# First quarter of the conditioning columns on TensorE, and filter steps issued ahead of it

## The chip, the cores and the metric

One core of a Trainium2 chip runs the program. The metric is device time in microseconds of the whole program, from three runs of each kernel. A profile of one further execution gives durations of single instructions; times inside it count from the start of its span.

## The reference

A trunk of two layers over 256 tokens of width 1024, all fp32. Of each layer only this matters here:

```
cond = silu(c)
ada  = cond @ w_ada[l] + b_ada[l]          # 6 x 1024: shift, scale, gate; twice
u    = x * (1 + scale1) + shift1
proj = u @ w_in[l]                         # attention, Hyena input, gates
filter: h = sin(freq0*(z@w1+b1)); h = sin(freq1*(h@w2+b2))
        h = (h@w3) * exp(-t * exp(log_decay)); normalised, then rfft
```

Attention, the Hyena convolution with these filters, the gates and a channel mixer over 16384 experts follow. The opening of layer 0 can make no u before the first columns of `ada` (shift and scale) are there.

## The kernel before

Weights come as tiles of 128x1024 from HBM on SP's queue (`raw`, three buffers, class `Stream`). ScalarE rounds each to `hi` (L88), VectorE or GpSimd (POOL) makes the rest `lo` (L90, by the letter "v" or "g" given in `plan`), and TensorE takes three products: hi with the high part of u, lo with it, hi with its low part (`tok_mm`, L211).

The opening is `start` (L276). It works in four quarters `kp` of the inner dimension, 256 rows of u each. A quarter's weights of `w_ada` for shift and scale are two tiles `su` of 1 MB (five buffers). For each quarter

* `sums` has VectorE multiply eight 128x512 pieces by one number of `cond` per partition and add them up into two accumulators (L293 twice, L296 six times);
* `columns` has TensorE turn the two accumulators, by products with the identity (L304, 8 matmuls, which the trace shows as 16 passes, since a fp32 matmul takes two), VectorE reduce them (L307) and add the bias (L309, `adac`);
* `u_part` (L479), called for both halves of the tokens, has TensorE turn x (L489), ScalarE make the high part (L492), and VectorE or ScalarE with POOL the low part `ul` (L497, L495, L500);
* `products(5, kp)` and `products(4, kp)` are the 12 matmuls each of two of the column chunks of `w_in`, numbers 5 and 4; chunk 4 comes one quarter late, between the next `columns` and its own `u_part`.

Between these stand steps of a generator, `filters` (L557), which `bg.pump` advances one yield at a time: the two sine layers (L584 on TensorE, seven small steps L587 to L593 on VectorE, L598 on ScalarE), then log_decay as a load spread over all partitions (1 MB) and its Exp (L610), eight products with w3 (L618) multiplied by the decays (L621, L623, L626), squares and their sums (L633 to L647), later the spectra (L676). What of it is not done in the opening goes on behind it, among chunks 0 to 3 of `w_in`.

Each engine works its instructions in the order of the program; the order is the one in which the Python code emits them, and the framework sets the waits. DMAs are issued by SP and by ScalarE's queue.

## Time and profile before

| | us |
|---|---|
| median of 3 runs | 2363.2 (2361.52 to 2363.59) |
| the profiled execution, its own time | 2362.55 |
| its span | 2360.4 |
| TensorE matmuls busy | 2267.1 |
| VectorE busy | 1789.6 |
| ScalarE busy | 1165.5 |
| POOL busy | 301.1 |

Durations and starts below are those of the profiled execution, whose span is 2.15 us shorter than its time. Matmuls are pipelined: a busy TensorE is not one at its peak, and a group of matmuls is read from the start of the first to the start of what follows. "PE" is TensorE, "DVE" VectorE, "ACT" ScalarE; a q behind the name is the engine's queue of DMA issues. An idle engine shows the releaser in brackets, with the idle time before it.

### The profile page before, as it was taken

To read this page: it belongs to the slowest core of one execution; us is meant where nothing else is said; L and a number is where in the kernel's file an instruction comes from. 1 tells how busy PE (TensorE), PEld (TensorE's weight loads), DVE (VectorE), ACT (ScalarE), POOL (GpSimd) and SP (SyncE) were. 2 spreads that over 40 slices of the span, in tenths; PEclk is the share of its full clock that TensorE was granted. 3 is DMA by queue.
4 is the path that set the end of the run, shared out by engine and by line. 5 is a ranking of instruction groups with operands and counts; after the bars stand their busy time and mean duration, and the time that the engine had idled before them with its cause. 6 is when DMAs were issued, how large, how long until landed. Compare 5 with 4: busy or idle time off the path is not lost.

```text
span 2360.4 us, 38122 instructions
## 1 busy us (share of the span) xinstructions
PE 2267.1 (96%) x14400; PEld 1998.4 (85%) x14400; DVE 1789.6 (76%) x3414; ACT 1165.5 (49%) x1850; POOL 301.1 (13%) x177
## 2 busy tenths in 40 slices
PE   6999988999999999999999999999999999999997
PEld 4688767999999988886777987799999999888786
DVE  6886797967778877778886858877777888755656
ACT  3544434555554544444455454555555554444443
POOL 3100004730000000003023000258000000000200
PEclk9999999999999999999999999999999999999999
DMA  8553554555555578888655424455555555766664
GB/s 289 178 171 102 182 202 154 168 179 166 166 167 164 162 242 265 269 268 266 219 189 185 133 93 149 163 155 178 171 168 163 168 164 185 236 193 195 213 200 149
DMA packets 132591, 438.43 MB, mean 186 GB/s; under 512 B 16369, under 2 KB 17741, under 8 KB 130360
## 3 DMA queue, kind: packets, MB, share of 16 engines
q1 hardware_dynamic: 103328, 377.01, 50.5%
q10 hardware_dynamic: 26968, 51.23, 6.3%
q0 software_dynamic: 2112, 7.77, 1.1%
q8 instruction: 113, 1.85, 0.3%
q14 instruction: 70, 0.57, 0.1%
HBM read 432.80 MB, written 3.15 MB: 185 GB/s over the span
## 4 chain that ended last, share of the span: by engine, by line
PE 77%; DVE 14%; ACT 3%; issue 3%; DMA 2%; POOL 0%; ACTq 0%; DVEq 0%
PE bg L223 33%; PE pj L1565 26%; PE pj L211 8%; DVE lo L90 4%; ACT hi L88 2%; PE gp L1463 1%; PE gp L1464 1%; PE pj L223 1%; PE bg L676 1%; DVE acc L432 1%; PE bg L618 1%; PE pj L1032 1%; PE pj L1376 1%; DMA raw<-in_wout 1%; DMA raw<-in_v 1%
## 5 line engine op out<-in xcount | busy, mean ns | idle before, releaser
L90 DVE TENSOR_TENSOR lo<-raw,hi 128x1024 fp32r<-128x1024 f32 x614 | 757.9, 1237 | 336.3 <-ACT hi L88 331.2
L88 ACT ACTIVATE hi<-raw 128x1024 fp32r<-128x1024 f32 x688 | 726.6, 1058 | 457.4 <-PE pj L1565 255.1
L1565 PE MATMUL pj<-hi,P 128*128 128x512 f32 x2048 | 638.8, 393 | 4.3 <-ACT P L1509 2.0
L223 PE MATMUL bg<-uh,hi 128*128 128x256 f32 x2240 | 640.8, 286 | 0.0
L223 PE MATMUL bg<-uh,lo 128*128 128x256 f32 x2240 | 634.1, 283 | 1.8 <-DVE lo L90 1.3
L223 PE MATMUL bg<-ul,hi 128*128 128x256 f32 x2240 | 633.3, 283 | 0.0
L1565 PEld LDWEIGHTS pj<-hi,P 128*128 128x128 f32 x2048 | 384.7, 189 | 90.2 <-ACT hi L88 3.4
L223 PEld LDWEIGHTS bg<-uh,lo 128*128 128x128 f32 x2240 | 429.2, 192 | 3.4 <-DVE lo L90 2.5
L223 PEld LDWEIGHTS bg<-ul,hi 128*128 128x128 f32 x2240 | 429.4, 192 | 0.1
L223 PEld LDWEIGHTS bg<-uh,hi 128*128 128x128 f32 x2240 | 429.3, 192 | 0.1
L1565 PE MATMUL pj<-lo,P 128*128 128x512 f32 x1024 | 401.7, 392 | 7.2 <-DVE lo L90 7.2
L1565 PEld LDWEIGHTS pj<-lo,P 128*128 128x128 f32 x1024 | 193.4, 189 | 51.7 <-DVE lo L90 11.6
L211 PE MATMUL pj<-hi,uh 128*128 128x512 f32 x432 | 189.9, 440 | 3.8 <-DVE mt L1189 2.3
L90 POOL TENSOR_TENSOR lo<-raw,hi 128x1024 fp32r<-128x1024 f32 x74 | 183.6, 2496 | 77.8 <-ACT hi L88 77.5
L1494 ACT ACTIVATE bg<-bg 128x8 f32<-128x8 f32 (+23 forms) x192 | 51.0, 266 | 268.1 <-PE bg L223 268.1
L211 PE MATMUL pj<-lo,uh 128*128 128x512 f32 x432 | 175.0, 405 | 7.2 <-DVE lo L90 7.2
L211 PE MATMUL pj<-hi,ul 128*128 128x512 f32 x432 | 174.9, 405 | 6.4 <-DVE ul L1249 5.7
L197 POOL DMA_DIRECT2D x<-spill x2 | 1.3, 649 | 1117.9 <-DVE P L1510 1117.9
L1470 DVE SCALAR_TENSOR_TENSOR b<-gp,b 128x160 f32<-128x160 f32 (+5 forms) x244 | 63.6, 322 | 97.0 <-ACT b L1468 97.0
L432 DVE SCALAR_TENSOR_TENSOR acc<-adaw,cond,acc 128x512 f32<-128x512 f32 x140 | 110.7, 791 | 0.0
L1079 POOL TENSOR_TENSOR e<-early,e 128x1024 fp32r<-128x1024 f32 x12 | 30.9, 2573 | 620.0 <-ACT e L1078 620.0
L211 PEld LDWEIGHTS pj<-hi,uh 128*128 128x128 f32 x432 | 84.4, 195 | 29.1 <-issue 7.4
(317 smaller groups left out, 2856.2 us busy)
## 6 DMA issues: line engine op xcount, KB each, us to landing
raw<-in_u SPq DMA_DIRECT2D x256, 512.0 KB, 3.6
raw<-in_v SPq DMA_DIRECT2D x256, 512.0 KB, 4.3
raw<-in_wtok SPq DMA_DIRECT2D x92, 512.0 KB, 3.7
adaw<-in_wada ACTq DMA_DIRECT2D x160, 256.0 KB, 4.0
raw<-in_whyd SPq DMA_DIRECT2D x24, 512.0 KB, 3.6
raw<-in_wq SPq DMA_DIRECT2D x24, 512.0 KB, 3.7
raw<-in_wbr SPq DMA_DIRECT2D x20, 512.0 KB, 3.6
su<-in_wada SPq DMA_DIRECT2D x8, 1024.0 KB, 10.6
```

The costliest lines, as they stand in the source:

```text
L88: self.nc.scalar.activation(out=h, in_=t, func=AF.Copy)
L90: eng.tensor_tensor(out=w, in0=t, in1=h.bitcast(F32), op=ALU.subtract)
L211: self.nc.tensor.matmul(psums[T], l[:, k, s], m[:, kk, :], start=(k == 0 and j == 0), stop=(k == K - 1 and j == 2))
L223: self.nc.tensor.matmul(ps, m[:, k, :], x[:, k, :], start=(k == 0 and j == 0), stop=(k == 7 and j == 2))
L432: nc.vector.scalar_tensor_tensor(out=acc, in0=w, scalar=self.cond[:, k:k + 1], in1=acc, op0=ALU.mult, op1=ALU.add)
L618: nc.tensor.matmul(p, hcur[:, T * 128:T * 128 + 128], w3[:, n * 512:n * 512 + 512], start=True, stop=True)
L676: nc.tensor.matmul(ps[P], self.fwd[:, P, c, :], z[:, P, :], start=True, stop=True)
L1032: self.nc.tensor.matmul(ps[T], x[:, 2 * i + kk, ts], w[:, kk, :], start=x is self.uh and i + kk + part == 0, stop=x is self.ul and i + kk ...
L1079: self.nc.gpsimd.tensor_tensor(out=w, in0=t, in1=h.bitcast(F32), op=ALU.subtract)
L1470: nc.vector.scalar_tensor_tensor(out=t[:, :, ts], in0=pr[:, i:j, :], scalar=1.0 / GATE_UNIT, in1=t[:, :, ts], op0=ALU.mult, op1=ALU.mult)
L1494: nc.scalar.activation(out=p[:, 0:n], in_=p[:, 0:n], func=AF.Gelu)
L1565: self.nc.tensor.matmul(self.vacc[T][h], x[:, s], v[:, w], start=start and c == 0, stop=stop and c == 2)
```

## The change

For the first quarter VectorE's sums go. TensorE multiplies the `su` tiles as weights by one column of `cond` (L312, 32 matmuls of one column), and two additions on VectorE make `adac`. For the other quarters the accumulators are summed by a product with a column of ones (L307, 8 matmuls) in place of the turning and the reduce. The log-decay is loaded as one row and spread by four products with a row of ones (L602), each followed by an Exp. Filter steps are advanced by two before the first quarter, by one in it and by two more ahead of each quarter's products. `products(4, kp)` comes right behind `products(5, kp)` and the next `sums`. All low parts of u go to VectorE, as do the two first splits of `w_in` tiles; the other six go to POOL. Only two `raw` tiles are loaded ahead of x. The layer's constants are loaded in quarters 2 and 3.

```diff
--- before.py
+++ after.py
@@ -61,8 +61,8 @@
         self.items.append((key, ap, split, own))
         self.ring.append(self.ring[-1] + (not own))
 
-    def _load(self):
-        while self.n_load < min(self.n_split + self.bufs + self.spare, len(self.items)):
+    def _load(self, most=1000):
+        while self.n_load < min(self.n_split + self.bufs + self.spare, len(self.items), most):
             here = self.where[self.n_split:].count(self.raw_pool) < self.bufs
             self.where.append(self.raw_pool if here else self.own)
             t = self.where[-1].tile([128, 1024], F32, tag="raw", name="raw", bufs=self.bufs if here else self.spare)
@@ -255,6 +255,8 @@
         self.load(self.ident, a["ident"])
         self.bcol = c.tile([128, DEPTH, 6, 8], F32, name="bcol")
         self.load(self.bcol, a["bada"])
+        self.one = c.tile([128, 128], F32, name="one")
+        nc.vector.memset(self.one, 1.0)
         self.new_x()
         self.open_layer(0)
         self.cond = c.tile([128, 8], F32, name="cond")
@@ -297,16 +299,24 @@
                                                        op0=ALU.mult, op1=ALU.add)
                 return acc
 
-            def columns(kp, acc):
-                q = self.bp((128, 4, 128))
+            def columns(kp):
+                q = self.bp((128, 2, 4))
                 for m in range(4):
-                    for i in range(2):
-                        nc.tensor.matmul(q[:, m, :], acc[i][:, m * 128:m * 128 + 128], self.ident,
-                                         start=(i == 0), stop=(i == 1))
-                p = self.sm.tile([128, 2, 2], F32, tag="ac0", name="ac0")
-                nc.vector.tensor_reduce(out=p.rearrange("p j k -> p (j k)"), in_=q, op=ALU.add, axis=AX.X)
+                    ms = slice(m * 128, m * 128 + 128)
+                    for i in range(2 if kp else 0):
+                        nc.tensor.matmul(q[:, 0, m:m + 1], acc[i][:, ms], self.one[:, 0:1], start=(i == 0),
+                                         stop=(i == 1))
+                for i in range(0 if kp else 2):
+                    for m in range(4):
+                        for kk in range(4):
+                            nc.tensor.matmul(q[:, i, m:m + 1], tiles[i][:, kk, m * 128:m * 128 + 128],
+                                             self.cond[:, 4 * i + kk:4 * i + kk + 1], start=(kk == 0), stop=(kk == 3))
                 ks = slice(2 * kp, 2 * kp + 2)
-                nc.vector.tensor_tensor(out=self.adac[:, 0, 0:2, ks], in0=p, in1=self.bcol[:, 0, 0:2, ks], op=ALU.add)
+                p = self.adac[:, 0, 0:2, ks]
+                q = q.rearrange("p i (j k) -> p i j k", j=2)
+                nc.vector.tensor_tensor(out=p, in0=q[:, 0], in1=self.bcol[:, 0, 0:2, ks], op=ALU.add)
+                if not kp:
+                    nc.vector.tensor_tensor(out=p, in0=q[:, 1], in1=p, op=ALU.add)
 
             def load_x(kp):
                 s = slice(kp * 256, kp * 256 + 256)
@@ -315,33 +325,37 @@
             load()
             load()
             load_x(0)
-            st._load()
+            st._load(2)
             for kp in range(1, 4):
                 load_x(kp)
                 load()
             pairs = {n: self.pair() for n in (5, 4)}
             loads = self.layer_loads(0)
-            st.run(3)
-            acc = sums(0)
+            self.bg.pump(2)
+            st.run(2)
 
             def products(n, kp):
                 self.tok_mm(pairs[n], self.uh, self.ul, st.get(("tok", 0, n, kp)), 2 * kp, 2, 8)
                 self.bg.pump()
-                next(loads, None)
+                if kp > 1:
+                    next(loads, None)
+                    next(loads, None)
 
             for kp in range(4):
-                columns(kp, acc)
+                columns(kp)
+                if kp == 0:
+                    self.bg.pump()
                 for T in range(2):
-                    self.u_part(T, 2 * kp, "va"[T], "vg"[T])
+                    self.u_part(T, 2 * kp, "va"[T], "v")
+                self.bg.pump(2)
+                for _ in range((2, 1, 0, 0)[kp]):
+                    load()
+                products(5, kp)
                 if kp < 3:
                     acc = sums(kp + 1)
-                for _ in range((2, 1, 0, 0)[kp]):
-                    load()
-                if kp:
-                    products(4, kp - 1)
-                self.bg.pump()
-                products(5, kp)
-            products(4, 3)
+                products(4, kp)
+            for _ in loads:
+                pass
         return pairs
 
     def new_x(self):
@@ -361,7 +375,7 @@
             if l == 0:
                 for kp in range(4):
                     for n in (5, 4):
-                        st.add(("tok", l, n, kp), a["wtok"][l, n, kp], "g")
+                        st.add(("tok", l, n, kp), a["wtok"][l, n, kp], "g" if kp else "v")
                 tok(0, 1, 2, 3)
             else:
                 tok(5, 4, 1, 2, 3)
@@ -576,8 +590,17 @@
             self.load(nt, a["negt"])
             w3 = fp.tile([64, 2048], F32, name="w3")
             ld = fp.tile([128, 2048], F32, name="ld")
+            if l == 0:
+                row = free[0:1, 1024:3072]
+                self.load(row, a["log_decay"][l:l + 1])
+                self.load(w3, a["hy_w3"][l])
             for _ in range(3 if l else 1):
                 yield
+            if l == 0:
+                for n in range(4):
+                    p = self.bp()
+                    nc.tensor.matmul(p, self.one[0:1, :], row[:, n * 512:n * 512 + 512], start=True, stop=True)
+                    nc.scalar.activation(out=ld[:, n * 512:n * 512 + 512], in_=p, func=AF.Exp)
             hcur, wcur = zt, w1
             for i in range(2):
                 p = self.bp((64, 256))
@@ -600,14 +623,13 @@
                 if l:
                     yield
                 hcur, wcur = h, w2
-            self.load(w3, a["hy_w3"][l])
             if l:
+                self.load(w3, a["hy_w3"][l])
                 yield
-            n = 1024 if l else 2048
-            for i in range(0, 2048, n):
-                self.load(ld[:, i:i + n], a["log_decay"][l][i:i + n].partition_broadcast(128))
-                yield
-            nc.scalar.activation(out=ld, in_=ld, func=AF.Exp)
+                for i in range(0, 2048, 1024):
+                    self.load(ld[:, i:i + 1024], a["log_decay"][l][i:i + 1024].partition_broadcast(128))
+                    yield
+                nc.scalar.activation(out=ld, in_=ld, func=AF.Exp)
             sums = fp.tile([128, 2, 4], F32, name="sums")
             yield
             todo = None
```

Line numbers of the changed kernel: L312 and L307 are the matmuls in `columns`, L317 and L319 its additions, L295 and L298 the sums, L602 the spreading of log-decay, L640 and L645 (L648 the last) the products with w3, L503, L506, L511 and L514 the steps of `u_part`, L610 to L616 the argument steps of a sine.

**TensorE, from its first instruction.** Before (acc are the accumulators of the first quarter):

```order
L304 MATMUL bg<-ident,acc_176 128x128
L304 MATMUL bg<-ident,acc_177 128x128
L304 MATMUL bg<-ident,acc_176 128x128
L304 MATMUL bg<-ident,acc_177 128x128
L304 MATMUL bg<-ident,acc_176 128x128
L304 MATMUL bg<-ident,acc_177 128x128
L304 MATMUL bg<-ident,acc_176 128x128
L304 MATMUL bg<-ident,acc_177 128x128
L489 MATMUL bg<-ident,x 128x128 x4
L584 MATMUL bg<-hh,w_109 64x256
L211 MATMUL pj<-hi,uh 128x512
```

With the change (hh holds the row of log-decay, one the ones, w_111 and w_113 are the filter's w1 and w2):

```order
L602 MATMUL bg<-hh,one 128x512 x4
L607 MATMUL bg<-hh,w_111 64x256
L312 MATMUL bg<-cond,su 128x1 x32
L607 MATMUL bg<-h_181,w_113 64x256
L503 MATMUL bg<-ident,x 128x128 x4
L211 MATMUL pj<-hi,uh 128x512
```

Five products of the filter now stand ahead of the first columns, and another between them and the first turned x.

**VectorE, from the second filter product or reduce of a quarter to the next quarter's sums.** Before, around the third quarter (acc_380 is an accumulator of the fourth):

```order
L307 TENSOR_REDUCE ac_359<-bg 128x4
L309 TENSOR_TENSOR adac<-ac_359,bcol 128x2x2
L497 TENSOR_SCALAR uft<-bg,adac 128x128 x2
L500 TENSOR_TENSOR ul<-uft,uh 128x2x128
L293 TENSOR_SCALAR acc_380<-su,cond 128x512
```

With the change, around the second quarter (acc_287 is an accumulator of the second quarter, acc_379 of the third):

```order
L298 SCALAR_TENSOR_TENSOR acc_288<-su,cond,acc_288 128x512
L645 TENSOR_TENSOR hh<-bg,hh 128x512
L317 TENSOR_TENSOR adac<-bg,bcol 128x2x2
L511 TENSOR_SCALAR uft<-bg,adac 128x128 x2
L514 TENSOR_TENSOR ul<-uft,uh 128x2x128 x2
L645 TENSOR_TENSOR hh<-bg,hh 128x512 x3
L295 TENSOR_SCALAR acc_379<-su,cond 128x512
```

The reduce is gone; a second ul and three products of the filter have come between the columns and the next sums.

**POOL, from the start.** Before:

```order
L90 TENSOR_TENSOR lo<-raw,hi 128x1024 x3
L500 TENSOR_TENSOR ul<-uft,uh 128x2x128 x2
L90 TENSOR_TENSOR lo<-raw,hi 128x1024 x2
L500 TENSOR_TENSOR ul<-uft,uh 128x2x128
L90 TENSOR_TENSOR lo<-raw,hi 128x1024 x2
L994 CAST iota<-iota_437 128x128
L500 TENSOR_TENSOR ul<-uft,uh 128x2x128
L90 TENSOR_TENSOR lo<-raw,hi 128x1024
```

With the change:

```order
L90 TENSOR_TENSOR lo<-raw,hi 128x1024 x5
L649 MEMSET hh 1x1024
L90 TENSOR_TENSOR lo<-raw,hi 128x1024
L1016 CAST iota<-iota_559 128x128
L1114 MEMSET kT 128x3584
```

Three of the eight splits before are ready at the first quarter; of the six now, two belong to each of the later quarters.

## Rows read from the trace of the kernel before

**Rows 1.** The page, the chain that ended last, shares by engine.

```profile
PE 77%; DVE 14%; ACT 3%; issue 3%; DMA 2%; POOL 0%; ACTq 0%; DVEq 0%
```

**Rows 2.** Busy time by stretch: us, engines, granted clock, DMA share, GB/s.

```profile
14.00:16.00 2.00, 2.00 (x9) 1.84 (x10) 0.36 (x1) 1.63 (x2) 1.35 (x1) 1.00 1.03 368
...
20.00:40.00 20.00, 15.07 (x59) 10.53 (x60) 18.38 (x31) 6.50 (x14) 5.55 (x4) 1.00 0.97 385
...
40.00:42.00 2.00, 1.94 (x9) 1.70 (x10) 1.86 (x6) 0.00 (x0) 0.00 (x0) 0.53 0.00 0
```

**Rows 3.** Timeline, TensorE and VectorE, turned sums and stored columns (start, us, what).

```profile
13.75 4.02 PE L304 MATMUL bg<-ident,acc 128*128 128x128 f32 x16 [13.75 <-DVE acc L296]
18.53 0.82 DVE L309 TENSOR_TENSOR adac<-ac,bcol 128x4 f32<-128x4 f32 x1
26.64 2.40 PE L304 MATMUL bg<-ident,acc 128*128 128x128 f32 x16
30.55 0.16 DVE L309 TENSOR_TENSOR adac<-ac,bcol 128x4 f32<-128x4 f32 x1
39.86 3.87 PE L304 MATMUL bg<-ident,acc 128*128 128x128 f32 x16 [3.99 <-DVE acc L296]
44.50 0.16 DVE L309 TENSOR_TENSOR adac<-ac,bcol 128x4 f32<-128x4 f32 x1
55.29 2.05 PE L304 MATMUL bg<-ident,acc 128*128 128x128 f32 x16
58.11 0.16 DVE L309 TENSOR_TENSOR adac<-ac,bcol 128x4 f32<-128x4 f32 x1
```

**Rows 4.** Timeline, TensorE, the narrowest fp32 matmuls that the trace has.

```profile
159.13 1.00 PE L823 MATMUL bg<-v,pt 128*128 128x64 f32 x8
```

**Rows 5.** Timeline, POOL, two splits of the opening.

```profile
34.13 2.38 POOL L90 TENSOR_TENSOR lo<-raw,hi 128x1024 fp32r<-128x1024 f32 x1 [0.20 <-ACT hi L88]
...
48.68 2.36 POOL L90 TENSOR_TENSOR lo<-raw,hi 128x1024 fp32r<-128x1024 f32 x1 [0.21 <-ACT hi L88]
```

**Rows 6.** VectorE groups by line, 34.9 to 35.6, then 23.3 to 24.0.

```profile
L296 DVE SCALAR_TENSOR_TENSOR acc<-su,cond,acc 128x512 f32<-128x512 f32 x1 | 2.9, 2924 | 0.0
...
L296 DVE SCALAR_TENSOR_TENSOR acc<-su,cond,acc 128x512 f32<-128x512 f32 x2 | 1.4, 742 | 0.0
```

**Rows 7.** Chain of waits in order of time, 55 to 80 us (start, us).

```profile
60.52 1.91 PE bg L618 x4
...
66.42 2.96 PE pj L211 x12
69.38 1.05 PE bg L618 x2
...
74.66 1.05 PE bg L618 x2
```

**Rows 8.** Timeline, VectorE, ScalarE and its queue, single steps.

```profile
6.15 0.36 ACTq L197 DMA_DIRECT2D nt<-in_negt  x1
...
27.08 0.53 DVE L587 TENSOR_SCALAR hh<-bg,col 64x256 f32<-64x256 f32 x1
29.63 0.28 DVE L593 TENSOR_SCALAR hh<-hh 64x256 f32<-64x256 f32 x1
43.49 1.04 ACT L88 ACTIVATE hi<-raw 128x1024 fp32r<-128x1024 f32 x1
43.80 0.60 ACTq L197 DMA_DIRECT2D ld<-in_log_decay  x1
47.07 0.42 DVE L500 TENSOR_TENSOR ul<-uft,uh 128x256 fp32r<-128x256 f32 x1
66.55 1.23 DVE L90 TENSOR_TENSOR lo<-raw,hi 128x1024 fp32r<-128x1024 f32 x1 [0.55 <-ACT hi L88]
67.69 0.68 DVE L623 TENSOR_TENSOR hh<-bg,hh 128x512 f32<-128x512 f32 x1
```

**Rows 9.** DMA issues, 0 to 80 us: nt, its KB and the us to landing.

```profile
nt<-in_negt ACTq DMA_DIRECT2D x1, 1.0 KB, 1.7
```

## The prediction

> **What bounds the kernel now.** I read the chain of waits first, for the whole span and then for the opening. Over the span it is 77% TensorE [rows 1], all engines are in-order, and nothing later waits for a fixed hour: a shift of the opening should reach the end almost whole. So the question is when the opening ends. The stretches come second: the transfers fill 0.97 of the DMA engines from 20 to 40 us, but nothing moves from 40 to 42 us [rows 2], while two of the four quarters are still to come; the weights are not the pace there. The timeline names the pace [rows 3]. Four times TensorE turns VectorE's sums (L304), VectorE stores the columns (L309), and only then can the next quarter of u be made. The columns are stored at 19.35, 30.71, 44.66 and 58.27 us (start plus duration). From 55 to 78 us the chain stays on TensorE without a gap, and its last products of the opening end at 69.38 us [rows 7].
>
> **The first quarter.** Sums(0) on VectorE and L304 go. In their place stand, one behind the other on TensorE: the log-decay row, four L602, one L607 and 32 L312.
>
> The row for L602 is issued on ScalarE's queue behind nt, which was issued at 6.15 to 6.51 us and took 1.7 us to land [rows 8, 9]; behind it that gives 8.3 us. (This issue and that of w3, at most 0.60 us each by [rows 8], also put the conditioning vector at most 1.2 us later. It is wanted only by L312, so that is hidden.)
>
> L602 is a fp32 matmul of 512 columns, as L618, of which two take 1.91 us [rows 7], 0.95 each. That is at TensorE's upper pace. L304 shows two paces: 4.02 us for 16 passes in the first quarter, 2.05 us in the fourth [rows 3]. The clock row reads 0.53 beside the 3.87 us of the third quarter; beside the first it reads 1.00, though the passes are as slow [rows 2, 3], so here I go by durations: half pace, 1.2 GHz, at first. Four L602 at half pace are 4 x 0.95 x 1.96 = 7.4 us, L607 with half the columns 0.9 us: 16.6 us.
>
> L312 has one column. Its price is not in the trace. The nearest row has 64 columns: 8 passes in 1.00 us [rows 4], 0.125 each, as much as the 0.128 of L304's 128 columns. Narrow matmuls are not cheaper; every pass has its own 128x128 weight load. 32 matmuls of two passes are 64 passes: 8.2 us at the upper pace, 16.1 at half.
>
> In the kernel before, TensorE ran at half pace from its first matmul at 13.75 until about the second L304, which is fast at 26.64 [rows 3]. I let it run as long at half pace here: 8.3 + 12.9 = 21.2. So 4.6 us of L312 at 0.25 are 18 passes and the other 46 take 5.9: 27.1, and two small additions, 0.16 each plus hand-over, 27.6 us. Against 19.35 that is **+8.2 us**. Bounds: upper pace throughout, 8.3 + 3.8 + 0.5 + 8.2 + 0.5 = 21.3 (+2); half pace throughout, 33.2 (+14). The other engines would not allow much below 24: L610 to L616, seven steps worth 2.83 us (27.08 to 29.91), two L88 of 1.04 and two splits of 1.23 now stand ahead of L317 [rows 8].
>
> **The second quarter**, 11.36 us before. The argument steps lie beside VectorE's sums in both kernels and cancel. New: both w_tok splits of a quarter are now on POOL during the sums. Such a split takes 2.4 us [rows 5], and the accumulation that met one took 2.92 us where its neighbours take 0.74 [rows 6]: VectorE stood still, 2.2 us a time. Before, the second quarter met none, the third and fourth one each. Now I count two in each: +4.4. The second ul moves from POOL to VectorE, 0.42 [rows 8]. L307 has as many passes as L304, so 2.05 us, and it is no longer covered by the argument steps, which now come ahead of the sums: +2.05, less 0.7 for the reduce that stood between L304 and L309 [rows 3]. **+6.2 us.**
>
> **The third quarter.** One more hold, +2.2; ul, +0.4; three L645 of 0.68 [rows 8] now stand between ul and the sums, +2.0; the reduce, -0.7. TensorE idled ahead of L304 here and went to half pace (3.87 us); it will idle again, so L307 costs as much. **+3.9 us.** **The fourth** is the same less the L623 that stood ahead of its reduce, 0.7: **+3.2 us.** The columns are then stored at about 28, 45, 63 and 80 us.
>
> **After the fourth quarter**, 69.38 - 58.27 = 11.1 us before, with two sets of products, L618 and the last set behind. Now: ul is ready 2.83 us after the columns (44.66 to 47.49 [rows 3, 8]), the first set runs into that and ends after some 4.8 us, the second 2.96 later [rows 7]: 7.7. **-3.4 us.**
>
> **Filter steps that no longer follow.** Three L618 behind the opening, 1.05 us each, on the chain [rows 7], and three L623 and L626 of 0.68 us on VectorE [rows 8]: 5.2 at most, 2.0 at least. I take **-5.0**; the squares are the same work a little earlier. Hidden at no cost: Exp in four pieces (ScalarE idles), the one-column memset, the layer's constants issued later (wanted by rope, which comes later too), the raw tiles and su tiles behind them on SP: su for quarter 3 is asked for when L312 ends, near 28 us, and wanted near 50. If that cover were gone, the next late thing would be that tile.
>
> **Sum:** 8.2 + 6.2 + 3.9 + 3.2 - 3.4 - 5.0 = +13.1 us. The profiled execution took 2362.55 us (span 2360.4); its time is 0.65 us below the median of the runs, which is within their spread. 2362.55 + 13.1 = **2375.7 us, slower.** The forecast's own range takes the first quarter at 24 instead of 27.6 (-3.6) and one hold fewer in two quarters (-4.4), or half pace through most of L312 (+5) and through two L307 (+4): 2367 to 2385.
>
> **Rivals.**
>
> *Columns of one are nearly free.* If a one-column pass cost only its issue, L312 would end with the splits on VectorE, at 24 us (-3.6), and L307 would save up to 2.05 us three times (-6.2): +3.3, 2365.9 us, within 0.2%. For it: nothing in the trace is narrower than 64 columns. Against: 64 columns cost what 128 do [rows 4]. The Trainium skill ("TensorE: Matmul & The Clock Gate", section "Wait — 56ns, not 53.3ns?") states that start-to-start never falls below about 25 ns however narrow a matmul is; 64 passes would then be 1.6 us, an estimate, and the total about this rival's. The same page (section "LDWEIGHTS (loading the stationary operand)") prices a weight load by its columns over 1.2, 107 ns for 128, and the 0.125 us of [rows 4] sides with that one. Chance 0.08.
>
> *POOL's splits miss the sums.* They start when ScalarE has made hi, and ScalarE now has Exp steps in front. Each hold that falls elsewhere gives back 2.2 us; without the four added ones, +13.1 - 8.8 = +4.3, about 2366.9 us. For: order on ScalarE is tight. Against: the sums last 5 us and more, and the splits come right behind uh and two Exp in each quarter. In part (two missed, 2371) it lies in my range. Chance of all four 0.09.
>
> *VectorE is what the opening waits for, and it is relieved* (faster). Sums(0), 5 us, and four reduces of 0.7 leave VectorE. If sums(1) could run while L312 does, the second quarter would come at its old 30.7 us, and the quarters after it no later than before; then the -3.4 and -5.0 remain: 2354.2 us. It decides if the fourth columns stand before 58.27 + 8.4 = 66.7 us. For it: TensorE waited 4.0 us for such sums ahead of the third quarter [rows 3]. Against: on VectorE's order sums(1) stands behind the splits, both ul and the second argument steps, all after L317. Chance 0.08.
>
> *Everything cancels* by smaller gains of several of these: within 0.2%. Chance 0.05.
>
> **Numbers.** The forecast has 0.70, all of it slower. By over 0.2% (4.7 us, about what a measurement of this kernel tells from no change) slower: forecast 0.70 and about half of the missed splits, 0.05, 0.75; within: 0.08 + 0.04 + 0.05 = 0.17; faster 0.08. The range reaches from the narrow-column rival's low side to the forecast's upper end: 2364 to 2386.
>
> **What would show it.** L317 at about 28, 45, 63 and 80 us; 64 passes of L312 at 0.11 to 0.25 us; two L298 of nearly 3 us in each quarter's sums; the last product of chunk 4 near 88 us; no L640 behind it. It is wrong if L312 takes under 3 us, if the fourth columns stand before 67 us, or if the difference at the end of the opening does not live on to the end of the span.

## The result and the profile after

The changed kernel takes 2377.8 us (median of 4 runs, 2372.65 to 2380.98) against 2362.36 us beside it: ratio 1.0067, 95% interval 1.0053 to 1.0081, about 15.4 us slower. The forecast was 2375.7 us. Its direction and nearly its size hold; the terms do not all.

The page of the changed kernel, the chain that ended last by engine, answers to [rows 1]:

```profile
PE 76%; DVE 14%; ACT 4%; issue 3%; DMA 2%; POOL 0%; ACTq 0%; DVEq 0%
```

TensorE's share is nearly the same (76% against 77%). The opening itself follows. First the timeline of TensorE in the changed kernel (start, duration, engine, line, operation, count, and in brackets the idle time before and what ended it):

```profile
10.59 7.16 PE L602 MATMUL bg<-hh,one 1*128 1x512 f32 x8 [10.59 <-DMA hh<-in_log_decay]
...
18.72 13.81 PE L312 MATMUL bg<-cond,su 128*128 128x1 f32 x64
...
38.61 0.53 PE L211 MATMUL pj<-lo,uh 128*128 128x512 f32 x1
38.98 0.39 PE L211 MATMUL pj<-hi,ul 128*128 128x512 f32 x1
...
45.22 1.95 PE L307 MATMUL bg<-one,acc 128*128 128x1 f32 x16
```

TensorE does not rest from 10.6 to 32.5 us, and yet L312 takes 0.216 us a pass to its end. The pace rises only at 38.6 us, 4 us into the 512-column products, which began at 34.7. At 45 us a one-column pass then costs 0.12 us (L307), nearly as much as the 0.128 us of L304's with 128 columns [rows 3]: width is not the price. (The pace does not stay: the granted clock is 0.50 again from 49 to 56 us.)

The stretch of L312 by windows (busy time of TensorE, its weight loads, VectorE, ScalarE and POOL, then the granted clock, the DMA share and GB/s):

```profile
18.00:32.00 14.00, 14.00 (x65) 13.28 (x63) 5.00 (x9) 3.98 (x5) 0.00 (x0) 1.00 1.02 410
```

Every pass has its own weight load, and the loads are busy for 13.28 of the 14.00 us. The clock reads 1.00 beside L312, as it did beside the slow first L304 [rows 2, 3]. Ahead of its first recorded change it can't be trusted; the passes' own spacing can.

The timeline of VectorE in the changed kernel, with the sums (L295, L298) and the ends of the first and fourth columns (L319, L317), and below it POOL's splits (L90):

```profile
32.77 0.16 DVE L319 TENSOR_TENSOR adac<-bg,adac 128x4 f32<-128x4 f32 x1
...
39.58 0.87 DVE L295 TENSOR_SCALAR acc<-su,cond 128x512 f32<-128x512 f32 x2
40.37 4.05 DVE L298 SCALAR_TENSOR_TENSOR acc<-su,cond,acc 128x512 f32<-128x512 f32 x6
...
51.90 3.09 DVE L295 TENSOR_SCALAR acc<-su,cond 128x512 f32<-128x512 f32 x2
54.91 6.19 DVE L298 SCALAR_TENSOR_TENSOR acc<-su,cond,acc 128x512 f32<-128x512 f32 x6
...
80.67 0.16 DVE L317 TENSOR_TENSOR adac<-bg,bcol 128x4 f32<-128x4 f32 x1 [2.12 <-PE bg L307]
...
41.13 7.81 POOL L90 TENSOR_TENSOR lo<-raw,hi 128x1024 fp32r<-128x1024 f32 x2 [40.69 <-DVE acc L298]
51.93 2.37 POOL L90 TENSOR_TENSOR lo<-raw,hi 128x1024 fp32r<-128x1024 f32 x1 [2.99 <-ACT hi L88]
```

The columns are stored at 32.93, 47.37, 63.82 and 80.83 us, against 19.35, 30.71, 44.66 and 58.27 [rows 3]. In the second quarter no sum is held: two L295 in 0.87, six L298 in 4.05 us. It was POOL that stood still there: asked for at 41.1, its two splits of 2.4 us took 7.81, and some 3 us of that lie beside the sums, which end at 44.3. In the third quarter (and so in the fourth, 3.46 and 6.16 us) each of the two groups of sums is held, by 2.1 to 2.6 us.

The chain of waits of the changed kernel from the sine of the second quarter's filter steps to the sums of the fourth quarter (start, length, engine, line):

```profile
39.69 0.43 ACT h L621
...
40.16 1.12 PE bg L640 x2
41.28 2.96 PE pj L211 x12
...
45.29 1.88 PE bg L307 x16
...
49.11 2.07 PE bg L640 x2
51.18 5.18 PE pj L211 x12
...
57.42 2.94 PE pj L211 x12
...
61.42 2.21 PE bg L307 x16
...
69.09 3.37 DVE acc L295 x2
...
73.04 5.51 DVE acc L298 x5
```

Up to the third columns the chain waits for no sum. In the second quarter the chain runs over the filter steps, the sine and TensorE's queue, in which L307 stands behind two sets of products. In the third it is TensorE alone, one set of products at half pace (5.18 us against 2.94); its held sums end at 61.10 us, 0.3 us before TensorE is free for L307. VectorE's holds decide in the fourth quarter only.

Last, the source view of L223, the first matmuls behind the opening's projections and the filter work, between 130 and 170 us, in the kernel before and in the changed one (first and last start stand after the durations):

```profile
L223 PE MATMUL pj<-uh,hi x58: 277/283/470, 138.5 to 169.0; 128*128 128x256 f32 x58
```

```profile
L223 PE MATMUL pj<-uh,hi x32: 278/283/365, 154.0 to 169.3; 128*128 128x256 f32 x32
```

154.0 - 138.5 = 15.5 us: as much as the whole difference of the medians is there at 140 us. How far it lives on shows in the source view of a later line, a product of the expert stages of both layers (L1565, in the changed kernel L1587):

```profile
L1565 PE MATMUL pj<-hi,P x2048: 387/389/793, 840.9 to 2347.9; 128*128 128x512 f32 x187
```

```profile
L1587 PE MATMUL pj<-hi,P x2048: 387/389/793, 857.1 to 2358.4; 128*128 128x512 f32 x187
```

Its first start, in layer 0, is still 16.2 us late, its last, at the end of layer 1, only 10.5. So in this pair of executions some 5 us go between 842 and 1592 us, where the program is the same. From the chain of waits that stretch takes 741.1 to 750.3 us in the fourteen executions profiled here, and the kernel before's is the longest. The medians, 15.4 us apart, do not show such a loss.

### The profile page after: what moved, and what is told of

Read it like the earlier page. It is cut to its first block, busy times and chain, and to the rows that moved or that the text cites. A ratio compares the mean times of both kernels' runs of the same rounds, so it can differ in the third digit from the quotient of the medians.

```text
span 2370.9 us, 38225 instructions
## 1 busy us (share of the span) xinstructions
PE 2286.6 (96%) x14456; PEld 2010.7 (85%) x14456; DVE 1787.9 (75%) x3410; ACT 1165.8 (49%) x1853; POOL 299.3 (13%) x171
## 4 chain that ended last, share of the span: by engine, by line
PE 76%; DVE 14%; ACT 4%; issue 3%; DMA 2%; POOL 0%; ACTq 0%; DVEq 0%
PE bg L223 32%; PE pj L1587 25%; PE pj L211 8%; DVE lo L90 4%; ACT hi L88 2%; PE gp L1485 1%; PE gp L1486 1%; PE pj L223 1%; PE bg L698 1%; DMA raw<-in_v 1%; DVE acc L446 1%; PE bg L640 1%; PE pj L1398 1%; PE bg L312 1%; PE pj L1054 1%
## 5 line engine op out<-in xcount | busy, mean ns | idle before, releaser
L90 DVE TENSOR_TENSOR lo<-raw,hi 128x1024 fp32r<-128x1024 f32 x616 | 760.9, 1238 | 333.8 <-ACT hi L88 327.4
L1587 PE MATMUL pj<-hi,P 128*128 128x512 f32 x2048 | 637.3, 392 | 6.1 <-ACT hi L88 2.7
L223 PE MATMUL bg<-uh,hi 128*128 128x256 f32 x2240 | 640.7, 286 | 0.0
L223 PE MATMUL bg<-uh,lo 128*128 128x256 f32 x2240 | 634.1, 283 | 1.9 <-DVE lo L90 1.3
L223 PE MATMUL bg<-ul,hi 128*128 128x256 f32 x2240 | 633.3, 283 | 0.0
L1587 PEld LDWEIGHTS pj<-hi,P 128*128 128x128 f32 x2048 | 383.9, 188 | 91.1 <-ACT hi L88 4.7
L223 PEld LDWEIGHTS bg<-uh,lo 128*128 128x128 f32 x2240 | 429.0, 192 | 3.5 <-DVE lo L90 2.6
L223 PEld LDWEIGHTS bg<-ul,hi 128*128 128x128 f32 x2240 | 429.3, 192 | 0.1
L223 PEld LDWEIGHTS bg<-uh,hi 128*128 128x128 f32 x2240 | 429.2, 192 | 0.1
L1587 PE MATMUL pj<-lo,P 128*128 128x512 f32 x1024 | 401.1, 392 | 5.2 <-DVE lo L90 5.2
L1587 PEld LDWEIGHTS pj<-lo,P 128*128 128x128 f32 x1024 | 192.8, 188 | 50.2 <-DVE lo L90 10.2
L90 POOL TENSOR_TENSOR lo<-raw,hi 128x1024 fp32r<-128x1024 f32 x72 | 183.1, 2559 | 109.4 <-ACT hi L88 68.4
```

The costliest lines, as they stand in the source:

```text
L90: eng.tensor_tensor(out=w, in0=t, in1=h.bitcast(F32), op=ALU.subtract)
L223: self.nc.tensor.matmul(ps, m[:, k, :], x[:, k, :], start=(k == 0 and j == 0), stop=(k == 7 and j == 2))
L1587: self.nc.tensor.matmul(self.vacc[T][h], x[:, s], v[:, w], start=start and c == 0, stop=stop and c == 2)
```

## The experiments

Every run is given by where its first and fourth columns are stored, by the shift of that first L223 against 138.5 us, and by its median against the runs of the kernel before beside it.

| kernel | first columns | fourth columns | shift of L223 | median less before | ratio, 95% interval |
|---|---|---|---|---|---|
| before | 19.35 | 58.27 | 0 | 0 | 1 |
| changed | 32.93 | 80.83 | +15.5 | +15.4 | 1.0053 to 1.0081 |
| e1 sums back | 25.36 | 72.87 | +8.6 | +9.0 | 1.0021 to 1.0046 |
| e2 filters behind | 24.48 | 83.69 | +20.6 | +19.7 | 1.0061 to 1.0112 |
| e3 64 columns | 32.61 | 80.00 | +16.6 | +15.9 | 1.0040 to 1.0089 |
| e4 warm | 30.19 | 77.42 | +12.8 | +12.2 | 1.0040 to 1.0080 |
| e5 before, ones | 17.54 | 61.09 | +5.6 | +2.8 | 0.9998 to 1.0027 |
| e6 sums first | 32.79 | 86.45 | +22.4 | +21.2 | 1.0062 to 1.0115 |
| e7 splits on VectorE | 32.98 | 79.47 | +14.3 | +16.5 | 1.0047 to 1.0097 |
| e8 before, ones, warm | 16.05 | 57.12 | -0.8 | +3.7 | 1.0007 to 1.0034 |
| e9 first splits | 18.01 | 55.74 | +1.0 | +0.5 | 0.9990 to 1.0020 |
| e10 kept wide | 17.53 | 56.25 | +1.1 | +1.0 | 0.9985 to 1.0016 |
| e11 all splits | 17.24 | 54.93 | -2.5 | -2.9 | 0.9973 to 1.0002 |
| e12 early w3 | 17.42 | 57.54 | +3.1 | +0.9 | 0.9984 to 1.0009 |

The shift and the difference of the medians agree within 1 us in eight of the thirteen changed kernels, and within 4.5 us in all: what the opening does at 140 us is, by and large, what the kernel does. The shift comes from one execution, the median from 4 to 12, so a difference of a few us between them is the spread of executions.

**e1: the first quarter on VectorE again.**

```
-            self.bg.pump(2)
+            acc = sums(0)
+            self.bg.pump(2)
             st.run(2)
...
-                    for i in range(2 if kp else 0):
+                    for i in range(2):
...
-                            nc.tensor.matmul(q[:, i, m:m + 1], tiles[i][:, kk, m * 128:m * 128 + 128],
```

> The first quarter alone goes back to VectorE's sums (turned by a column of ones); all else is as in the changed kernel. Theory (the 64 one-column passes L312 at half pace, 13.8 us, are the loss of the first quarter): the columns wait for L607 at about 18.7 us and then 16 passes, 22.5 us, but VectorE has L610 to L616 and two splits in front of L317, so they are stored at about 26 us instead of 32.9; the later quarters keep their distance, and the whole is 6 to 8 us less than the changed kernel, about 2370 to 2372. Rival (the loss is the steps put in front, not L312): columns stay near 32 us, time within 2 us of the changed kernel's 2377.8.

Timeline of VectorE and TensorE in e1:

```profile
25.20 0.16 DVE L312 TENSOR_TENSOR adac<-bg,bcol 128x4 f32<-128x4 f32 x1
...
18.54 3.57 PE L307 MATMUL bg<-one,acc 128*128 128x1 f32 x16
```

The columns come 7.6 us earlier, behind VectorE's splits as expected, and 6.9 us of it are left at L223; the median is 9.0 us above before instead of 15.4. So L312 is worth 6.4 to 6.9 us, close to half of the loss. The other half, 8.6 us at L223, is the steps in front, the new order and the splits together. Of these the steps in front (with the two splits on VectorE) put the first columns at 25.36 us instead of 19.35; the rest was not taken apart.

**e2: the filter steps not in front.**

```
-            self.bg.pump(2)
             st.run(2)
```

> The filter steps (log-decay row, L602, L607) no longer stand in front of the columns; L312 stays. Theory: L312 starts near 10.5 us, when the conditioning vector and the first tile are there, still takes 13 to 14 us at half pace, and the columns are stored at about 25 us instead of 32.9; L602 and L607 then stand between the columns and the first products and take back 4 to 5 us of that, and two more filter steps follow the opening, 2 us: 1 to 3 us less than the changed kernel, 2375 to 2377. Rival (L602 and L607 are the loss and cost nothing elsewhere): 8 us less, about 2370.

Timeline of TensorE and VectorE in e2:

```profile
10.27 13.81 PE L312 MATMUL bg<-cond,su 128*128 128x1 f32 x64 [10.27 <-DVE cond L267]
24.01 7.19 PE L601 MATMUL bg<-hh,one 1*128 1x512 f32 x8
...
32.17 1.11 PE L502 MATMUL bg<-ident,x 128*128 128x128 f32 x4
...
33.74 0.73 DVE L510 TENSOR_SCALAR uft<-bg,adac 128x128 f32<-128x128 f32 x2 [9.26 <-ACT uh L505]
```

L312 is the same 13.81 us eight us earlier, again at half pace throughout, so the steps in front did not slow it. But L601 and L606 (L602 and L607 of the changed kernel) now stand on TensorE ahead of the transposes that u needs, and VectorE waits 9.26 us for them. Both expectations are wrong: no gain but a further 5 us lost at L223. Given L312, the steps in front are the better order.

**e3: 64 equal columns in place of one.**

```
-                            nc.tensor.matmul(q[:, i, m:m + 1], tiles[i]...
-                                             self.cond[:, 4 * i + kk:4 * i + kk + 1], ...
+                            nc.tensor.matmul(q[:, i, m, :], tiles[i]...
+                                             self.cond64[:, 4 * i + kk, :], ...
```

> Each L312 multiplies 64 equal columns instead of one (the vector copied 64 times on VectorE, 0.5 us); nothing else changes. Theory one (a pass costs its weight load, and width is free): 64 passes still take 0.213 us each at half pace, 13.8 us, time as the changed kernel within 2 us. Theory two (as one, and the wider work lets TensorE rise to 2.4 GHz during L312, as it rose 4 to 6 us after the first 512-column products in both kernels): L312 takes about 10 us, columns near 29 us, 3 to 4 us less in all. Rival (a pass costs its columns): over 0.25 us each at half pace, L312 over 16 us, 2 us slower or more.

Timeline of TensorE in e3 (L314 is the changed kernel's L312):

```profile
18.31 13.91 PE L314 MATMUL bg<-cond,su 128*128 128x64 f32 x64
```

13.91 against 13.81 us: theory one. Sixty-four times the columns cost 0.1 us, and did not raise the pace within 14 us either.

**e4: six wide matmuls of ones in front** (extra work, its sum unused).

```
+            for _ in range(6):
+                nc.tensor.matmul(pw, self.one, self.wide, start=True, stop=True)
             pairs = {n: self.pair() for n in (5, 4)}
```

> Six matmuls of ones (128 rows, 512 columns, fp32) run on TensorE ahead of L602, from about 1 us on; their sum is not used. Theory (TensorE is at 1.2 GHz in the opening because it has done no wide work yet): they begin at half pace, 1.7 us each, the pace rises after 4 to 6 us of them, L602 takes 3.6 instead of 7.2 us and L312 about 8 instead of 13.8; columns stored near 23 us instead of 32.9, and the whole about 9 us less than the changed kernel, about 2368 to 2369. Rival one (the pace rises at a fixed hour near 38 us, or falls again while L312 runs): L312 still takes 13 us or more, columns at 30 to 34 us, 2375 to 2379. Rival two (columns come near 23 us but a later wait takes the gain): columns early, time as the changed kernel.

Timeline of TensorE, and windows, in e4 (its L607 and L314 are L602 and L312 of the changed kernel):

```profile
1.59 7.50 PE L336 MATMUL bg<-wide,one 128*128 128x512 f32 x12 [1.59 <-DVE wide L261]
10.20 4.81 PE L607 MATMUL bg<-hh,one 1*128 1x512 f32 x8 [1.11 <-DMA hh<-in_log_decay]
...
15.98 13.81 PE L314 MATMUL bg<-cond,su 128*128 128x1 f32 x64
```

```profile
2.00:9.00 7.00, 7.00 (x12) 2.58 (x11) 0.00 (x0) 1.49 (x2) 0.00 (x0) 1.00 0.71 233
...
13.00:16.00 3.00, 3.00 (x6) 0.64 (x4) 0.00 (x0) 1.53 (x3) 0.00 (x0) 0.50 0.96 232
16.00:30.00 14.00, 14.00 (x66) 13.98 (x66) 5.16 (x10) 3.25 (x4) 0.00 (x0) 0.50 1.03 407
...
37.00:40.00 3.00, 3.00 (x12) 1.62 (x11) 3.00 (x6) 2.97 (x4) 1.60 (x1) 1.00 0.01 3
```

The clearest run. The pace does rise within the wide matmuls: 12 passes in 7.50 us, where at L602's 0.895 they would take 10.7. The one-row matmuls behind them still get 4.81 us instead of 7.16, and then the record shows 1.2 GHz (0.50) from 13 to 36 us, although TensorE is busy with one-row and one-column work up to 30 us; it shows 2.4 GHz again 4 to 5 us after the 512-column products begin at 32.0. L312 is 13.81 us to the hundredth. It is not a fixed hour, then: rival one's second form, the pace falls again. It fell 2.4 us into the one-row matmuls, ahead of which TensorE had rested for 1.1 us; which of the two let it fall was not separated. The 3 us gained are L602's and live on. As the same 13.81 us go with a recorded 0.50 here, the unrecorded half pace of L312 in the changed kernel is 1.2 GHz too.

**e5: the column of ones alone, on the kernel before.**

```
-                        nc.tensor.matmul(q[:, m, :], acc[i][:, m * 128:m * 128 + 128], self.ident,
+                        nc.tensor.matmul(q[:, m:m + 1], acc[i][:, m * 128:m * 128 + 128], self.one[:, 0:1],
...
-                nc.vector.tensor_reduce(out=p.rearrange("p j k -> p (j k)"), in_=q, op=ALU.add, axis=AX.X)
```

> The kernel before with one part of the change alone: the sums are turned by the one column instead of the identity, and the reduce goes. Theory (a pass costs its weight load however narrow, so only the reduce of 0.7 us a quarter leaves): the turn still takes about 3.6 us in the first quarter and 2 us in the last, columns stored about 0.7 us earlier in the first quarter, 1.5 to 3 us by the fourth, time 1 to 3 us below before, which is within what can be told from no change. Rival (one-column passes nearly free): the turns take under 0.6 us, columns 2 to 3 us earlier in each quarter, 6 to 10 us less.

Timeline of TensorE and VectorE in e5:

```profile
13.54 3.81 PE L306 MATMUL bg<-one,acc 128*128 128x1 f32 x16 [13.54 <-DVE acc L298]
...
20.04 3.44 DVE L295 TENSOR_SCALAR acc<-su,cond 128x512 f32<-128x512 f32 x2
...
49.34 8.35 DVE L298 SCALAR_TENSOR_TENSOR acc<-su,cond,acc 128x512 f32<-128x512 f32 x6
```

The first turn costs 3.81 us with one column, 4.02 with 128 [rows 3]. The reduce is gained, the first columns come 1.8 us earlier, and that moves VectorE's sums onto POOL's splits: two L295 of the second quarter take 3.44 us instead of 1.34, and six L298 of the fourth take 8.35 instead of 6.22, two holds. The second turn, fast before (2.40 [rows 3]), takes 3.71 us, at half pace. The theory holds for the price of a pass, not for the later quarters: the fourth columns come 2.8 us later. In the medians gain and loss end within what can be told from no change.

**e6: the next sums right behind u.**

```
                     self.u_part(T, 2 * kp, "va"[T], "v")
+                if kp < 3:
+                    acc = sums(kp + 1)
                 self.bg.pump(2)
...
-                if kp < 3:
-                    acc = sums(kp + 1)
```

> The changed kernel with VectorE's sums of the next quarter issued right behind u, ahead of the filter steps and the first products' splits (as the kernel before has them). Theory (the later quarters are paced by VectorE's order: filter steps L610 to L616 stand ahead of the second quarter's sums, three L645 of 0.68 us ahead of the others'): the second columns come 2 to 3 us earlier, the third and fourth 2 us more each, 4 to 7 us in all, about 2371 to 2374. Rival one (the filter steps so delayed follow behind the opening): columns earlier, but three L640 of 1.05 us behind it again, net within 2 us of 2377.8. Rival two (TensorE is the pace of the later quarters): columns as before the edit.

Timeline of VectorE and TensorE in e6:

```profile
37.46 4.05 DVE L298 SCALAR_TENSOR_TENSOR acc<-su,cond,acc 128x512 f32<-128x512 f32 x6
...
44.78 2.07 PE L640 MATMUL bg<-w,h 64*128 64x512 f32 x2 [4.04 <-ACT h L621]
52.63 2.19 PE L307 MATMUL bg<-one,acc 128*128 128x1 f32 x16
```

My theory falls, and none of the rivals was the one. The sums are ready at 41.5 us, three earlier, but L307 comes at 52.6, seven later. In TensorE's order it stands behind L640, which waits for the sine, whose argument steps now follow the sums on VectorE. TensorE idles 4.04 us, goes to half pace, and the second columns stand at 55 us instead of 47.4. This agrees with the chain shown above: the second quarter is paced by the filter steps and TensorE's queue.

**e7: no split on POOL.**

```
-                        st.add(("tok", l, n, kp), a["wtok"][l, n, kp], "g" if kp else "v")
+                        st.add(("tok", l, n, kp), a["wtok"][l, n, kp], "v")
```

> The changed kernel with every split of the opening on VectorE, none on POOL. Theory (a split on POOL holds a VectorE operation by 2.2 us, two a quarter in the third and fourth): no L295 or L298 over 1 us any more, each of these two quarters loses 4.4 us of holds and gains two splits of 1.23 us: 1.9 us less each; the second quarter, where POOL was the one held, gains 2.5 us; together 1 to 2 us less than the changed kernel by the fourth columns. Rival (the holds lie in idle time of VectorE): the third and fourth quarters become 2 us longer each, 4 to 7 us slower.

Timeline of VectorE in e7, third and fourth quarters:

```profile
57.84 4.05 DVE L298 SCALAR_TENSOR_TENSOR acc<-su,cond,acc 128x512 f32<-128x512 f32 x6
...
73.25 4.06 DVE L298 SCALAR_TENSOR_TENSOR acc<-su,cond,acc 128x512 f32<-128x512 f32 x6
```

The holds by POOL's splits are gone. The fourth columns come 1.4 us earlier and L223 1.2, as expected in sum, but not in its parts; the median cannot tell that from the changed kernel. The second columns stand at 49.77 us, 2.4 later, where an earlier time was expected: two splits of 1.23 us now stand in VectorE's order there. The third quarter is as long as before the edit (16.44 against 16.45 us), and the fourth is 3.8 us shorter. So the holds are real, but of the two quarters only the fourth pays for them, as the chain above has it.

**e8: e5 with eleven wide matmuls of ones in front.** The edit is that of e4 with 11 in place of 6, on e5.

> The one-column kernel of the previous kind (kernel before, column of ones, no reduce), with eleven 512-column matmuls of ones on TensorE from about 1.6 us on, until the sums of the first quarter are there. Theory (the pace follows wide full-row work and falls behind a stretch of single rows or columns, as in the run with six of them, where it rose within them and fell again at 12.6 us): the first turn, with no one-row work ahead of it, takes 2 us instead of 3.6, the first columns are stored near 16 us instead of 19.35, the first products run at 0.23 us instead of 0.43, and the whole is 2 to 5 us below before. Rival (the gain is cover for VectorE's sums): first columns 3 us earlier, fourth columns and the whole within 1 us of the one-column kernel without them.

Windows of e8:

```profile
18.00:35.00 17.00, 13.98 (x42) 10.67 (x41) 14.75 (x25) 6.17 (x13) 6.48 (x5) 0.51 1.02 414
```

The first columns come at 16.05 us, as the theory has it. Then, behind 5 us of gaps and one-column work, the clock is at 0.51 until 35 us, products included, and the second columns are at 30.3. The opening keeps its lead: the fourth columns come 4.0 us and L223 6.4 us earlier than in e5, which the rival did not expect. The whole does not gain, as the rival has it: the median lies 3.7 us above before. Of the 0.8 us that this execution is ahead of the kernel before at L223, nothing is left at 440 us, where the expert stage of layer 0 begins 2.0 us late. Why stays open.

**e9, e10, e11: towards a faster opening.** e9 is e5 with the first quarter's splits on VectorE, behind the first sums; e10 adds e8's eleven matmuls and three more between the first turn and the first products; e11 puts all the other splits but one on VectorE as well.

```
-            st.run(3)
-            acc = sums(0)
+            acc = sums(0)
+            st.run(3)
...
+                for _ in range(0 if kp else 3):
+                    nc.tensor.matmul(pw, self.one, self.wide, start=True, stop=True)
...
-                        st.add(("tok", l, n, kp), a["wtok"][l, n, kp], "g")
+                        st.add(("tok", l, n, kp), a["wtok"][l, n, kp], "g" if (kp, n) == (1, 5) else "v")
```

> Kernel before with the column of ones and no reduce, and the two splits of the first quarter on VectorE behind its first sums (as the changed kernel has them on VectorE) instead of POOL. Theory (in the one-column kernel POOL's split held the second quarter's L295, 3.44 us for two against 0.88): those two L295 take 0.9 us, the second columns come 1 to 2.5 us earlier, and 1 to 2.5 us live on to the end. Rival (the second columns wait for TensorE's products at half pace, not for the sums): columns at 30 to 31 us as without the edit, no difference.

> As the kernel with the first splits on VectorE, and TensorE kept on wide work: eleven matmuls of ones from 1.6 us to the first sums, three more between u's turn and the first products. Theory (after a gap and narrow work the pace fell at 18.2 us in the run with eleven alone; with no gap it stays): the first columns near 17 us, no low clock from 6 to 35 us, products of the first quarter at 0.23 us, the second turn 2 us instead of 3.7, second columns near 27 to 28 us, and 3 to 5 us below the kernel before. Rival (three more matmuls only delay the first products by 2.6 us and the clock falls all the same): second columns at 30 us or later.

> As the previous kernel with all splits of the opening but one on VectorE. Theory (a split on POOL costs VectorE 2.2 to 2.5 us where it meets a sum, on VectorE 1.23, and here it would fall behind the sums while TensorE turns them): no L297 or L300 over 1 us in the third and fourth quarters, each 1 to 2 us shorter, 1 to 3 us less than the previous kernel. Rival (ScalarE's hi comes late and VectorE, which works in order, waits for it ahead of the columns): third and fourth columns later, 0 to 4 us slower than the previous kernel.

Timeline of VectorE in e9, windows of e10, and timeline of VectorE and TensorE in e11:

```profile
20.32 1.35 DVE L295 TENSOR_SCALAR acc<-su,cond 128x512 f32<-128x512 f32 x2
```

```profile
16.00:24.00 8.00, 6.67 (x23) 3.36 (x21) 6.73 (x12) 4.75 (x9) 3.22 (x2) 1.00 1.03 412
24.00:35.00 11.00, 9.53 (x43) 7.74 (x44) 9.01 (x17) 3.56 (x8) 3.01 (x2) 0.84 1.03 416
```

```profile
32.97 4.05 DVE L300 SCALAR_TENSOR_TENSOR acc<-su,cond,acc 128x512 f32<-128x512 f32 x6
...
46.16 1.58 PE L626 MATMUL bg<-w,h 64*128 64x512 f32 x2 [2.51 <-DMA w<-in_hy_w]
```

In e9 the second quarter's hold is down from 2.6 to 0.5 us, and the second columns come 1.9 us earlier than before. In e10 the wide work keeps the clock at 1.00 to 24 us and mostly after it, but the second columns gain only 0.2 us more; TensorE waits 2.4 us for VectorE's sums ahead of that turn. In e11 no L300 is held, but only the fourth quarter is shorter than in e10, by 3.1 us. The third is 1.6 us longer: VectorE waits 1.43 us for ScalarE's hi and then does a split ahead of the columns, as the rival had it. The fourth columns are the earliest of all, 3.3 us ahead of the kernel before. Its median of 2356.5 us is clearly below the changed kernel's; against the kernel before the interval, 0.9973 to 1.0002, just touches no change.

**e12: e11 with w3 asked for early, as the change has it.**

```
             for _ in range(3 if l else 1):
                 yield
+            if l == 0:
+                self.load(w3, a["hy_w3"][l])
```

> As the kernel with nearly all splits on VectorE, and one more part of the change: the filter weights w3 are asked for ahead of the first filter matmul, not behind the second sine. Theory (in that kernel TensorE waited 2.51 us for this transfer ahead of the third quarter's first filter matmul, 43.7 to 46.2 us): the wait goes, the products behind it start 1.5 to 2.5 us earlier, the last product of chunk 4 falls from 66.4 to about 64.5 us, and the time is 4 to 5 us (0.15 to 0.2%) below the kernel before. Rival one (ul is what those products wait for: 46.8 us): gain under 0.5 us. Rival two (the transfer now takes room from the weights of the second quarter, whose tile VectorE already waited 0.73 us for): second columns 1 us later, no gain.

Timeline of VectorE in e12:

```profile
26.47 2.74 DVE L300 SCALAR_TENSOR_TENSOR acc<-su,cond,acc 128x512 f32<-128x512 f32 x4 [3.79 <-DMA su<-in_wada]
```

Rival two. The wait of e11 goes, but the 512 KB, issued at 17.7 us into transfers that fill the engines, bring the second quarter's su tile later: VectorE waits 3.79 us for it, and the second columns slip from 28.8 to 32.6. From 22 to 26 us the DMA engines are as full as in e11 (1.03 and 1.04) but move 223 GB/s instead of 414. The gain of e11 is gone.

## Why the prediction was right, and where it was not

The sum was +13.1; by its own steps the trace gives 13.6 + 3.1 + 2.5 + 3.4 - 1.8 - 5.3 = +15.5 us. That the two lie so close is in part luck: I had the first quarter 5.4 us too short and the second and third together 4.5 us too long.

- **First quarter, +8.2 forecast, +13.6 measured: the mis-sized term.** Of L312's 64 passes I put 18 at half pace and 46 at 0.128 us, on the ground that TensorE had risen some 13 us after its first matmul in the kernel before. That ground was wrong. TensorE rose behind the start of the 512-column products, 4 us here (34.7 to 38.6 us) and 7 us in the kernel before (19.95 to about 27 us, not the 4 to 6 in both that e3's text has), and in e4 it did not stay up through the one-row and one-column work. All 64 passes ran at half pace, 13.7 us from start to start instead of 10.5. Another 2.3 us I missed at the start: the row for L602, issued at 6.44 us, landed 4.0 us later, not 1.7 as nt [rows 9]. The columns at 32.93 us nearly meet my upper bound of 33.2, but that bound had 0.25 us for a half-pace pass, where L312 takes 0.215, and nothing for the late row.
- **Second quarter, +6.2 forecast, +3.1 measured.** Its mechanism was wrong. No sum was held: POOL's splits came while VectorE's sums ran back to back, and POOL stood still. I had priced one direction only; the traces show both (L296 held in [rows 6], POOL's two splits taking 7.81 us here). The Trainium skill ("SBUF — State Buffer", section "SBUF: two separate sides") says of the port pair that the two share that whichever starts first has it for the whole instruction and the other fully blocks. Both kinds of hold agree with that. The quarter's length comes from the argument steps, the sine and the queue on TensorE, as the chain and e6 show.
- **Third, +3.9 against +2.5, and fourth, +3.2 against +3.4.** Two holds a quarter are there as forecast. In the third they lie beside TensorE's queue, which ends last: the mechanism was wrong there too, and without the holds that quarter is as long (e7). In the fourth they are on the chain, and e7 gains 3.8 us there.
- **After the fourth, -3.4 against -1.8.** The first products of the last quarter ran at half pace up to 86.4 us, about nine passes 0.2 us longer each: 1.8 us.
- **Filter steps not following, -5.0 against -5.3.** The last product of chunk 4 stands 20.8 us late, L223 15.5. e1 shows the same 5 us given back (13.6 and 8.6 late); e5, where the filter steps are as before, gives back 0.3 (5.9 and 5.6).
- **The rivals.** "Nearly free" one-column passes: no; 0.12 us at the upper pace and 0.216 at the lower one, the same for 64 columns (e3). The Trainium skill ("TensorE: Matmul & The Clock Gate", section "LDWEIGHTS (loading the stationary operand)") prices a weight load at its columns over 1.2, which makes 107 ns for 128 columns, an estimate. The upper pace here is close to it, 0.113 us from start to start in L307 at 45 us; the lower is twice that. "VectorE is relieved": no; its sums of the second quarter began at 39.6 us, behind L319, as argued against it. Splits that miss the sums: true of one quarter, which came out 3.1 us below my forecast, not the 4.4 of two holds, since the sums were not what it waited for.

## What to carry to other kernels

A matrix-vector product on TensorE with the matrix as weights cost a full weight load per 128x128 block and pass here, as much for one column as for 64, and it ran at 1.2 GHz throughout; where VectorE would be idle anyway, its 5 us are cheaper than TensorE's 14. Price such work in a kernel's opening at the low pace, and take the pace from the spacing of passes, not from the clock record ahead of its first change. Where two engines hold each other, ask which one starts first, and look whether the held one is on the chain at all.

## What the hardware showed that was not expected

- The clock fell while TensorE worked: 0.50 recorded from 13 to 36 us in e4, with one-row and one-column matmuls back to back up to 30 us and no rest over 1.1 us before.
- Sixty-four columns instead of one cost 0.1 us over 64 passes and did not raise the pace (e3).
- POOL's split waited for several VectorE sums in a row, not for one: two splits of 2.4 us took 7.81.
- A transfer of 512 KB issued at 17.7 us and used at 46.5 cost 3.8 us elsewhere (e12); issued at 41.1 it had cost 2.5 (e11).
